# One of six low weight parts per expert step moved from VectorE to GpSimd

## The chip, the cores and the metric

One core of one Trainium2 chip runs the whole program. The metric is the device time of one execution in microseconds (us); less is better. The kernel before takes 1809.94 us (median of three runs, 1809.8 to 1809.99).

## The reference, cut to what matters

A hybrid block is followed by two more layers; the last of them ends in a mixture of experts. 256 tokens, 1024 wide, go through 8 experts of inner width 2816, and each token's two best experts count:

```python
def swiglu(x, w_gu, w_down):
    gu = jnp.einsum('bsd,df->bsf', x, w_gu)
    g, u = gu[..., :D_FF_2], gu[..., D_FF_2:]
    return jnp.einsum('bsf,fd->bsd', jax.nn.silu(g) * u, w_down)

def moe_swiglu(x, w_router, w_gu, w_down):
    ...
    for e in range(N_EXPERTS):
        out = out + gates[..., e:e + 1] * swiglu(x, w_gu[e], w_down[e])
    return out
```

All is float32. The kernel gets that precision from three fp32r products: every operand is split into a high part (rounded to fp32r) and a low part (the rest), and a product is high times high, plus low times high, plus high times low.

## The kernel before, in words

**The experts.** `expert` (L1579) runs once for each of 8 experts, 128 gathered tokens each, in 11 steps (j = 0 to 10) of 256 inner columns. A step reads three chunks of 1 MB from HBM with `load` (L181, issued by SP): two for gate and up weights, one for down weights. `split` (L187) makes two pairs from each chunk: the high part `wh` is a cast on ScalarE (L192), the low part `wl` is source minus high part on VectorE (L194), each 128x1024. So a step has six casts and six subtractions. The text calls the four pairs of the gate and up weights u0 to u3, and the two of the down weights d0 and d1; all six subtractions are VectorE's.

`up(j)` multiplies the tokens by u0 to u3 (24 matmuls of 512 columns, tile gu), takes silu on ScalarE (L1596), multiplies gate and up on VectorE (L1597, called mul below), transposes the product on TensorE (`tr`, L251) and splits it into hH (ScalarE, L1603) and hL (VectorE, L1604). `dnw` (L1607) loads and splits the down weights of the step before; `dn` (L1611) multiplies by them (12 matmuls, tile y; L241 is the one that reads a low part). An expert's last `dn` is run inside the next expert's first step, and its result goes through ScalarE (L1644) to HBM.

**Rings.** wh and wl live in five slots (rings "hl": 3 and 2), chunks in seven (rings "raw": 3, 1 and 3, after two lent ones are taken out in the first expert at JL = 8). A chunk's slot is free for the next load when its last reader, so far the subtraction of its second pair, is done.

**The gather.** Experts come in pairs. In experts 1, 3 and 5 the tokens of the next pair are gathered in four of the steps: matmuls into t (L1538, L1539), then xe on VectorE (L1543) and ScalarE (L1545, L1546), and its low part on GpSimd (L1547, 128x256, two in such a step). Besides these GpSimd has nothing to do in the experts, but for four indirect loads in the eighth (L1737).

**Order.** The order of the instructions on each engine is not written out: the program builder sorts them by its own estimate of when operands are ready, under the dependencies. `queue`, `behind` and `hold` add a few order constraints: `behind(..., 1)` keeps a subtraction on VectorE behind a held instruction; it acts while `held` is not used up, which is at the first few splits of a stage.

Of the kernel before, what the change touches and what calls it, by code (L numbers as in the profile page):

```python
# [8 lines left out]
F32 = mybir.dt.float32  # L9
# [108 lines left out]
def build(tc, a, out):  # L118
    nc = tc.nc
# [3 lines left out]
    def nm(s):  # L123
        uid[0] += 1
        return f"{s}_{uid[0]}"
# [21 lines left out]
    def slot(kind):  # L147

        p, taken = min(rings[kind], key=lambda x: x[1][0])
        count[0] += 1  # L150
        taken.append(count[0])
        taken.pop(0)
        return p
# [30 lines left out]
        nc.sync.dma_start(r[:, :n], ap.to_broadcast([128, n]) if ap.shape[0] == 1 else ap)  # L184
        return r

    def split(src):  # L187
        n = src.shape[-1]
        p = slot("hl")
        h = p.tile([128, CH // 2], F32R, tag="wh", name=nm("wh"))[:, :n]  # L190
        l = p.tile([128, CH // 2], F32R, tag="wl", name=nm("wl"))[:, :n]
        cast[0] = nc.scalar.copy(h, src)  # L192
        behind(cast[0], 0)
        behind(nc.vector.tensor_sub(l, src, h.bitcast(F32)), 1)  # L194
        count[1] += 1
        return h, l

# [9 lines left out]
    def behind(ins, i):  # L207
        if held[i] is not None and held[2] <= count[1]:
            queue(ins, held[i])
# [40 lines left out]
    def tr(o, i, k=128):  # L250
        nc.tensor.transpose(o, i, ident[:k, :k])  # L251
# [36 lines left out]
    with ExitStack() as st:  # L288
# [25 lines left out]
        for hf in range(2):  # L314
            c = slice(hf * 512, hf * 512 + 512)
# [41 lines left out]
    for k in range(8):  # L357
        if k % 2 == 0:
            h, l = split(bufs_[k // 4][:, (k % 4) * 280:(k % 4) * 280 + 560])
# [40 lines left out]
    for b in range(2):  # L400
# [3 lines left out]
        for h in range(8):  # L404
            o = bank("s", 3)
            r = slice(h % 2 * 64, h % 2 * 64 + 64)
# [15 lines left out]
        for kv in range(2):  # L422
# [3 lines left out]
            for i in range(4):  # L426
                h = kv * 4 + i
# [295 lines left out]
    for ch in (1, 2):  # L723
        c0 = BLK[ch][0]
# [40 lines left out]
    for ch in (1, 2):  # L765
        c0 = BLK[ch][0]
# [41 lines left out]
    for n in range(2):  # L808
        os_ = [bank("mm", 2) for _ in range(2)]
        for kg in range(2):  # L810
            r = load(a["w_z"][n * 2 + kg])
            for q in range(2):
                h, l = split(r[:, q * 1024:(q + 1) * 1024])
                for k2 in range(2):
                    k = kg * 4 + q * 2 + k2
                    s = slice(k2 * 512, k2 * 512 + 512)
                    for b in range(2):
                        c0 = BLK[b + 1][0]
# [474 lines left out]
    for b in range(2):  # L1293
        d = slice(b * 128, b * 128 + 128)
        o = bank("mm", 2)
        for k in range(8):
            h, l = hs[k // 2]
# [58 lines left out]
    for c in (0, 2):  # L1356
        hs = []
        for j in range(2):
            r = load(a["w_v"][c + j])
# [193 lines left out]
    made = pool("made", 1, bass.MemoryType.DRAM).tile([1024, D], F32, name="made")  # L1553
# [22 lines left out]
            nc.vector.tensor_reduce(rf, t, AX.X, ALU.add)  # L1576
            nc.vector.tensor_scalar_add(row[:, :, k], rf, C("own"))

    def expert(wap, xeH, xeL, c0, into=None, ST=None, gate=None, rest=None, ahead=(), final=False):  # L1579

        y = []

        def up(j):
            o = bank("gu", 2)
            for kg in range(2):
                r = load(wap(3 * j + kg))
                for q in range(2):
                    h, l = split(r[:, q * 1024:(q + 1) * 1024])  # L1590
                    for k2 in range(2):
                        k = kg * 4 + q * 2 + k2
                        s = slice(k2 * 512, k2 * 512 + 512)
                        xmm(o, xeH[:, k, c0:c0 + 128], xeL[:, k, c0:c0 + 128], h[:, s], l[:, s], k == 0, k == 7)
            g = ew.tile([128, 256], F32, tag="eg", name=nm("eg"))
            nc.scalar.activation(g, o[:, :256], AF.Silu)  # L1596
            mark[0] = nc.vector.tensor_mul(g, g, o[:, 256:])  # L1597
            t = bank("t", 2)
            for f in range(2):
                tr(t[:, f * 128:f * 128 + 128], g[:, f * 128:f * 128 + 128])  # L1600
            hH = ew.tile([128, 256], F32R, tag="hH", name=nm("hH"))
            hL = ew.tile([128, 256], F32R, tag="hL", name=nm("hL"))
            nc.scalar.copy(hH, t[:, :256])  # L1603
            nc.vector.tensor_sub(hL, t[:, :256], hH.bitcast(F32))  # L1604
            return hH, hL

        def dnw(j):  # L1607
            r = load(wap(3 * j + 2))
            return [split(r[:, f * 1024:(f + 1) * 1024]) for f in range(2)]

        def dn(j, hh, w=None, last=False):  # L1611
            w = w or dnw(j)
            if not y:
                y.extend(bank("y", 2) for _ in range(2))
            for f, n in ((0, 0), (1, 0), (0, 1), (1, 1)) if last else ((0, 0), (0, 1), (1, 0), (1, 1)):
                h, l = w[f]
                fs = slice(f * 128, f * 128 + 128)
                s = slice(n * 512, n * 512 + 512)
                xmm(y[n], hh[0][:, fs], hh[1][:, fs], h[:, s], l[:, s], j == 0 and f == 0, j == 10 and f == 1)

        pend = None
        for j in range(11):
            hh = up(j)
            w = dnw(pend[0]) if pend is not None else None
            if j < len(ahead):
                ahead[j]()
            if pend is not None:
                dn(*pend, w)
            pend = (j, hh)
            nj[0] += 1  # L1630
            if nj[0] == JL:
                rings["raw"][:] = [x for x in rings["raw"] if x not in lent]
            if rest is not None:
                rest(j)
        if final:
            dn(*pend, last=final)
            return y
        if into is not None:

            def store():  # L1640

                t = rowtile()
                for n in range(2):
                    queue(nc.scalar.copy(t[:, n * 512:n * 512 + 512], y[n]), cast[0])  # L1644
                nc.scalar.dma_start(into, t)

            return (lambda: dn(*pend)), store

        def sums(n):
            yy = rowtile().rearrange("p (i d) -> p i d", i=2).bitcast(F32R)  # L1650
            nc.scalar.copy(yy[:, 0], y[n])
            nc.vector.tensor_sub(yy[:, 1], y[n], yy[:, 0].bitcast(F32))
            s = slice(n * 512, n * 512 + 512)
            for b in range(2):
                o = bank("c", 2)
                for i in range(2):
                    mm(o, ST[:, b * 128:b * 128 + 128], yy[:, i], start=i == 0, stop=i == 1)
                nc.vector.scalar_tensor_tensor(x2[:, b, s], o, gate(b), x2[:, b, s], ALU.mult, ALU.add)

        return (lambda: dn(*pend)), (lambda: sums(0)), (lambda: sums(1))  # L1660
# [36 lines left out]
    left = ()  # L1697
# [8 lines left out]
    xe = tokens(0)  # L1706
    gather(*xe, S_, 2)
    for e in range(8):
        if e % 2 == 0 and e:
            xe, S_ = nxt  # L1710

        def rest(j, e=e):
            nonlocal nxt
            if e == 0 and j == 4:
                for n in range(2):
                    c = slice(n * 512, n * 512 + 512)
                    g, h = lnrow(0, n, "c"), lnrow(0, 2 + n, "c")
                    for b in range(2):
                        nc.vector.scalar_tensor_tensor(x2[:, b, c], xn[:, b, c], ALPHA, g, ALU.mult, ALU.mult)
                        nc.vector.scalar_tensor_tensor(x2[:, b, c], h, ALPHA, x2[:, b, c], ALU.mult, ALU.add)  # L1720
            if e == 1 and j < 4:
                nc.scalar.copy(gl_[:, j // 2, j % 2 * 512:j % 2 * 512 + 512], lnrow(1, j, "c"))

            if e % 2 and e < 7:
                if j == J0:
                    nxt = tokens(e + 1), ep.tile([128, 2, 2, 128], F32R, name=nm("S_"), tag="S", bufs=2)
                    onehot(nxt[1], pos, e + 1, 2)
                elif J0 < j <= J0 + 4:
                    k = 2 * (j - J0 - 1)
                    gather(*nxt[0], nxt[1], 2, k, k + 2)  # L1730
            if e == 2 and j == 0:
                places()

            if e == 7 and j in (2, 3, 6, 7):
                b, k = divmod(j - 2 if j < 4 else j - 4, 2)
                t = rowtile()
                nc.gpsimd.indirect_dma_start(t, None, made, bass.IndirectOffsetOnAxis(ap=row[:, b, k:k + 1], axis=0))  # L1737
                parts.append((b, k, t))
            if e == 7 and j in (5, 6, 9, 10):

                b, k, t = parts.pop(0)
                queue(nc.vector.scalar_tensor_tensor(x2[:, b], t, gk[:, b, k:k + 1], x2[:, b], ALU.mult, ALU.add), mark[0])
            if e == 6 and j == 5:
                o = bank("t", 2)
                for b in range(2):
                    sg = ew.tile([128, 128], F32, tag="sg", name=nm("sg"), bufs=1)
                    nc.vector.tensor_scalar_mul(sg, S_[:, b, 1].bitcast(F32), G[:, b, 7:8])
                    tr(o[:, b * 128:b * 128 + 128], sg)
                nc.scalar.copy(SG, o[:, :256])

        left = expert(lambda c, e=e: a["w_moe"][e * 33 + c], *xe, (e % 2) * 128, made[e * 128:e * 128 + 128], rest=rest, ahead=left, final=e == 7)
    y = left

    os_ = [bank(t, 2) for t in ("c", "c", "gu", "gu")]
# [15 lines left out]
    with tc.If(many > 128):  # L1770
# [3 lines left out]
        with tc.For_i(0, 8) as e:  # L1774
# [5 lines left out]
            xeH, xeL = [ew.tile([128, 8, 256], F32R, tag="xe" + n, name=nm("xe"), bufs=1) for n in "HL"]  # L1780
# [112 lines left out]
```

## Time and profile before

| | |
|---|---|
| median of runs | 1809.94 us |
| profiled execution, its own time | 1812.04 us |
| its span, first to last instruction | 1810.2 us |
| PE (matmul) busy | 1773.7 us, 98% |
| DVE (VectorE) busy | 1435.0 us, 79% |
| ACT (ScalarE) busy | 1129.9 us, 62% |
| POOL (GpSimd) busy | 136.0 us, 8% |
| the eight experts | from about 1012 to 1790 us of the span |
| granted TensorE clock, mean | 0.995 of 2.4 GHz |

The 88 steps of the experts are 43% of the span. An ordinary step lasts about 8.45 us, one with a gather about 9.7 us. A busy PE is a PE with a matmul in flight; matmuls overlap, so the spacing of their starts is what is read from a timeline.

### The profile page before, as it was taken

To read this page: it belongs to the slowest core of one execution; us is meant where nothing else is said; L and a number is where in the kernel's file an instruction comes from. 1 tells how busy PE (TensorE), PEld (TensorE's weight loads), DVE (VectorE), ACT (ScalarE), POOL (GpSimd) and SP (SyncE) were. 2 spreads that over 40 slices of the span, in tenths; PEclk is the share of its full clock that TensorE was granted. 3 is DMA by queue.
4 is the path that set the end of the run, shared out by engine and by line. 5 is a ranking of instruction groups with operands and counts; after the bars stand their busy time and mean duration, and the time that the engine had idled before them with its cause. 6 is when DMAs were issued, how large, how long until landed. Compare 5 with 4: busy or idle time off the path is not lost. (4 is left out here: it accounts for less than half of the span.)

```text
span 1810.2 us, 27298 instructions
## 1 busy us (share of the span) xinstructions
PE 1773.7 (98%) x10377; PEld 1515.8 (84%) x10377; DVE 1435.0 (79%) x2129; ACT 1129.9 (62%) x1704; POOL 136.0 (8%) x136
## 2 busy tenths in 40 slices
PE   9999999999999999999999899999999999999997
PEld 7978989999998898999977687888878787878775
DVE  6887886676666767555687999898989898989897
ACT  4477654564444655444454788887787777777775
POOL 2411220000000000000011200100010000100010
PEclk9999999999999999999999999999999999999999
DMA  6433331465554465553344689999999999999992
GB/s 224 171 102 113 105 137 61 176 250 202 186 186 166 166 218 224 209 189 137 117 163 164 239 334 373 331 365 347 374 353 355 361 379 366 349 354 377 366 414 94
DMA packets 64457, 443.45 MB, mean 245 GB/s; under 512 B 7952, under 2 KB 8368, under 8 KB 12608
## 3 DMA queue, kind: packets, MB, share of 16 engines
q1 hardware_dynamic: 59904, 430.04, 63.8%
q10 hardware_dynamic: 3840, 9.51, 1.4%
q8 instruction: 83, 1.36, 0.3%
q0 software_dynamic: 576, 2.10, 0.3%
q14 instruction: 54, 0.44, 0.1%
HBM read 436.37 MB, written 5.24 MB: 244 GB/s over the span
## 5 line engine op out<-in xcount | busy, mean ns | idle before, releaser
L194 DVE TENSOR_TENSOR wl<-raw,wh 128x1024 fp32r<-128x1024 f32 (+2 forms) x815 | 975.2, 1228 | 197.8 <-ACT wh L192 191.7
L192 ACT CAST wh<-raw 128x1024 fp32r<-128x1024 f32 (+2 forms) x815 | 824.6, 1047 | 338.1 <-PE mm L235 203.0
L239 PE MATMUL gu<-wh,xe 128*128 128x512 f32 x704 | 277.1, 394 | 0.8 <-DVE xe L1543 0.8
L240 PE MATMUL gu<-wh,xe 128*128 128x512 f32 x704 | 276.1, 392 | 1.3 <-POOL xe L1547 1.3
L241 PE MATMUL gu<-wl,xe 128*128 128x512 f32 x704 | 276.3, 393 | 0.0
L234 PE MATMUL mm<-xh,wh 128*128 128x256 f32 x592 | 168.2, 284 | 0.1
L235 PE MATMUL mm<-xl,wh 128*128 128x256 f32 x592 | 167.2, 282 | 0.0
L236 PE MATMUL mm<-xh,wl 128*128 128x256 f32 x592 | 166.7, 282 | 0.0
L241 PEld LDWEIGHTS gu<-wl,xe 128*128 128x128 f32 x704 | 132.2, 188 | 30.6 <-DVE wl L194 2.0
L240 PEld LDWEIGHTS gu<-wh,xe 128*128 128x128 f32 x704 | 132.3, 188 | 30.2 <-POOL xe L1547 2.7
L239 PEld LDWEIGHTS gu<-wh,xe 128*128 128x128 f32 x704 | 132.5, 188 | 27.4 <-DVE xe L1543 1.2
L239 PE MATMUL y<-wh,hH 128*128 128x512 f32 x352 | 139.3, 397 | 4.8 <-ACT yo L1644 4.8
L240 PE MATMUL y<-wh,hL 128*128 128x512 f32 x352 | 139.8, 397 | 0.0
L241 PE MATMUL y<-wl,hH 128*128 128x512 f32 x352 | 135.3, 405 | 0.0
L234 PEld LDWEIGHTS mm<-xh,wh 128*128 128x128 f32 x592 | 112.6, 190 | 4.4 <-issue 3.6
L235 PEld LDWEIGHTS mm<-xl,wh 128*128 128x128 f32 x592 | 112.4, 190 | 1.2 <-issue 0.8
L236 PEld LDWEIGHTS mm<-xh,wl 128*128 128x128 f32 x592 | 112.4, 190 | 0.0
L1596 ACT ACTIVATE eg<-gu 128x256 f32<-128x256 f32 x88 | 33.6, 382 | 107.6 <-PE gu L241 107.6
L234 PE MATMUL mm<-xTH,wh 128*128 128x256 f32 (+1 forms) x344 | 99.6, 290 | 0.6 <-DVE ct L384 0.5
L235 PE MATMUL mm<-xTL,wh 128*128 128x256 f32 (+1 forms) x344 | 98.8, 287 | 0.0
L236 PE MATMUL mm<-xTH,wl 128*128 128x256 f32 (+1 forms) x344 | 98.4, 286 | 0.0
L241 PE MATMUL acc<-wl,uh 128*128 128x512 f32 x216 | 85.1, 394 | 0.0
(573 smaller groups left out, 3275.8 us busy)
## 6 DMA issues: line engine op xcount, KB each, us to landing
raw<-w_moe SPq DMA_DIRECT2D x264, 1024.0 KB, 6.3
raw<-w_gud SPq DMA_DIRECT2D x33, 1024.0 KB, 4.8
raw<-w_ffn SPq DMA_DIRECT2D x32, 1024.0 KB, 4.8
raw<-w_wf SPq DMA_DIRECT2D x27, 1024.0 KB, 4.8
raw<-w_a SPq DMA_DIRECT2D x10, 1024.0 KB, 4.9
raw<-w_br SPq DMA_DIRECT2D x8, 1024.0 KB, 4.8
raw<-w_o SPq DMA_DIRECT2D x8, 1024.0 KB, 4.8
raw<-w_b SPq DMA_DIRECT2D x7, 1024.0 KB, 4.7
```

The lines of the kernel that those rows point to most:

```text
L192: cast[0] = nc.scalar.copy(h, src)
L194: behind(nc.vector.tensor_sub(l, src, h.bitcast(F32)), 1)
L234: mm(o, h[:, k], xh[:, k, ts], start=k == 0, stop=False)
L235: mm(o, h[:, k], xl[:, k, ts], start=False, stop=False)
L236: mm(o, l[:, k], xh[:, k, ts], start=False, stop=k == 7)
L239: mm(o, xh, h, start=first, stop=False)
L240: mm(o, xl, h, start=False, stop=False)
L241: mm(o, xh, l, start=False, stop=last)
L1596: nc.scalar.activation(g, o[:, :256], AF.Silu)
```

## The change

`split` gets a flag by which the subtraction goes to GpSimd; `dnw` sets it for the second half of the chunk (f = 1, so d1), and the caller for experts 0 to 6. `behind` is not called for it. Nothing else in the source is changed.

```diff
-    def split(src):
+    def split(src, pool=False):
...
-        behind(nc.vector.tensor_sub(l, src, h.bitcast(F32)), 1)
+        if pool:
+            nc.gpsimd.tensor_sub(l, src, h.bitcast(F32))
+        else:
+            behind(nc.vector.tensor_sub(l, src, h.bitcast(F32)), 1)
...
-    def expert(wap, xeH, xeL, c0, into=None, ST=None, gate=None, rest=None, ahead=(), final=False):
+    def expert(wap, xeH, xeL, c0, into=None, ST=None, gate=None, rest=None, ahead=(), final=False, third=False):
...
-            return [split(r[:, f * 1024:(f + 1) * 1024]) for f in range(2)]
+            return [split(r[:, f * 1024:(f + 1) * 1024], f == 1 and third) for f in range(2)]
...
-        left = expert(lambda c, e=e: a["w_moe"][e * 33 + c], *xe, (e % 2) * 128, made[e * 128:e * 128 + 128], rest=rest, ahead=left, final=e == 7)
+        left = expert(lambda c, e=e: a["w_moe"][e * 33 + c], *xe, (e % 2) * 128, made[e * 128:e * 128 + 128], rest=rest, ahead=left, final=e == 7, third=e < 7)
```

## Rows read from the trace of the kernel before

**Rows 1.** Busy time of each engine by stretch: early steps, one late step, gather step, step with expert change
```profile
core 0: us, PE busy (x) PEld busy (x) DVE busy (x) ACT busy (x) POOL busy (x), PEclk, DMA share, GB/s
1179.80:1222.30 42.50, 42.50 (x191) 34.31 (x190) 39.76 (x41) 34.06 (x41) 0.00 (x0) 1.00 0.97 373
1306.30:1314.80 8.50, 8.50 (x40) 6.96 (x40) 7.81 (x9) 6.49 (x9) 0.00 (x0) 1.00 0.97 372
1343.10:1352.80 9.70, 9.70 (x48) 7.68 (x47) 8.51 (x10) 7.89 (x11) 2.56 (x2) 1.00 0.89 329
1314.80:1324.50 9.70, 8.75 (x40) 6.87 (x39) 7.97 (x10) 7.87 (x12) 0.00 (x0) 1.00 0.93 344
```

**Rows 2.** Waits from 1100 to 1800 us: us in total, times, longest us
```profile
ACT eg L1596 <- PE gu L241: 107.6, 66, 3.5
...
PEld y L239 <- ACT yo L1644: 6.9, 5, 1.4
PE y L239 <- ACT yo L1644: 4.8, 5, 1.0
...
PEld gu L241 <- DVE wl L194: 2.0, 7, 0.4
...
PEld y L241 <- DVE wl L194: 0.8, 4, 0.2
```

**Rows 3.** Timeline of an ordinary late step: start us, us, engine, line, xcount, idle before
```profile
1306.58 3.90 ACT L192 CAST wh<-raw 128x1024 fp32r<-128x1024 f32 x4
...
1307.67 4.63 DVE L194 TENSOR_TENSOR wl<-raw,wh 128x1024 fp32r<-128x1024 f32 x4
...
1312.29 1.99 ACT L192 CAST wh<-raw 128x1024 fp32r<-128x1024 f32 x2
...
1312.42 0.42 DVE L1597 TENSOR_TENSOR eg<-eg,gu 128x256 f32<-128x256 f32 x1
...
1313.36 2.36 DVE L194 TENSOR_TENSOR wl<-raw,wh 128x1024 fp32r<-128x1024 f32 x2 [0.51 <-ACT wh L192]
...
1314.10 0.40 PE L241 MATMUL y<-wl,hH 128*128 128x512 f32 x1
```

**Rows 4.** GpSimd's timeline in the experts: two subtractions of 128x256
```profile
1161.99 0.74 POOL L1547 TENSOR_TENSOR xe<-eg,xe 128x256 fp32r<-128x256 f32 x1 [6.34 <-ACT eg L1546]
...
1346.78 1.82 POOL L1547 TENSOR_TENSOR xe<-eg,xe 128x256 fp32r<-128x256 f32 x1 [1.60 <-ACT eg L1546]
```

**Rows 5.** VectorE beside them: hL at 1161.89, and L194 from 1200 to 1400 us (min/median/max)
```profile
1161.89 0.42 DVE L1604 TENSOR_TENSOR hL<-t,hH 128x256 fp32r<-128x256 f32 x1
...
L194 DVE TENSOR_TENSOR wl<-raw,wh x136: 1207/1218/1765, 1198.8 to 1399.4; 128x1024 fp32r<-128x1024 f32 x136
```

**Rows 6.** Timeline, GpSimd's 128x512 operations in an earlier stage, and VectorE beside the second
```profile
217.20 1.28 POOL L740 TENSOR_TENSOR kT<-kT,t 128x512 f32<-128x512 f32 x1
...
265.90 1.22 DVE L194 TENSOR_TENSOR wl<-raw,wh 128x1024 fp32r<-128x1024 f32 x1
...
266.06 2.21 POOL L826 TENSOR_TENSOR zg<-zg,rows 128x512 f32<-128x512 f32 x1 [0.73 <-DVE zg L825]
```

**Rows 7.** Timeline of a late gather step
```profile
1345.19 0.54 DVE L1543 TENSOR_SCALAR xe<-t,ge 128x256 fp32r<-128x256 f32 x1 [1.19 <-PE t L1539]
...
1347.92 2.90 DVE L194 TENSOR_TENSOR wl<-raw,wh 128x1024 fp32r<-128x1024 f32 x2
...
1351.00 0.19 PEld L241 LDWEIGHTS y<-wl,hH 128*128 128x128 f32 x1
```

**Rows 8.** Timeline of an ordinary early step
```profile
1203.68 0.39 PE L241 MATMUL y<-wl,hH 128*128 128x512 f32 x1
...
1204.37 2.50 DVE L194 TENSOR_TENSOR wl<-raw,wh 128x1024 fp32r<-128x1024 f32 x2
...
1207.29 5.34 DVE L194 TENSOR_TENSOR wl<-raw,wh 128x1024 fp32r<-128x1024 f32 x4
```

**Rows 9.** Loads (L184) from 1200 to 1700 us, from issue to landing
```profile
DMA to landing us min/median/max: 4.7/6.5/8.7
```

## The prediction

> **What bounds the kernel now.** I read the stretches of the experts first, because the change touches nothing else. In early steps and in an ordinary late step PE is busy for the whole stretch, with VectorE at 39.76 of 42.50 us and 7.81 of 8.50 us [rows 1]. The waits say the same: ScalarE waits 107.6 us for PE, VectorE's subtractions make PE wait 2.0 us (gu) and 0.8 us (y) in 700 us, and the one large wait of PE is for ScalarE's copy of y, five times [rows 2]. So PE is the bound, and VectorE, 92% busy, is hidden. Taking work from VectorE can return the 2.8 us of the two small waits at most, unless the order of the queues changes with it. What has to be asked is whether the new GpSimd work stays hidden too.
>
> **What is removed.** 77 subtractions (7 experts of 11 steps) leave VectorE. One is 1.22 us long, and 1.14 us apart in a run of four, (4.63 - 1.22) / 3 [rows 3]. That frees some 1.14 us of each step on an engine that does not bound: worth 0 to 2.8 us in all.
>
> **What is added: 77 GpSimd subtractions of 128x1024.** No row shows one. By length: 0.74 us for 256 columns with no rival [rows 4] and 1.28 us for 512 [rows 6], so 0.54 us for each 256 and 1.28 + 2 x 0.54 = 2.36 us alone. By what it takes from VectorE: the 256-column one at 1346.78 lasted 1.82 us, not 0.74, since it had to let the VectorE subtraction in flight end [rows 4]; then the longest VectorE subtraction came to 1.765 us against a median of 1.218 [rows 5]. The two don't run beside each other: one holds the other off for its whole length, 0.55 us for 256 columns, so 2.19 us for 1024. The 512-column one at 266.06 ended at 268.27, 1.15 us after VectorE's subtraction at 265.90 (end 267.12) [rows 6], which makes 2.30 us for 1024. I take 2.2 us (the row with the same operation in the same stage), bounds 2.19 and 2.36 us. An operation that reads one of its inputs from PSUM isn't held off: hL took 0.42 us beside a GpSimd subtraction that took its 0.74 us [rows 4, 5]; mul, one input from PSUM as well, counts likewise.
>
> The Trainium skill (GPSIMD Engine Reference, "Key points") states that GpSimd shares its SBUF interfaces with VectorE and conflicts with VectorE instructions that have two SBUF inputs; rows 4 and 5 agree, with 1.82 against 0.74 us. The same page (section "Engine selection") says to keep elementwise work on VectorE, as about 2 times slower on GpSimd; by that rule the change loses, which is the second rival below.
>
> **An ordinary late step** (experts 2 to 6, no gather). VectorE's order is u0, u1, hL, u2, u3, d0, d1, mul. The run of four from 1307.67 is u2 to d1, so d0 ends at about 1311.16 and d1 at 1312.30; its cast ends at 1310.48, and PE reads d1 first at 1314.10 [rows 3], its weights some 0.23 us (one matmul's spacing) before. GpSimd would begin when d0 lets go, 1311.16, and end at 1313.36. That is 0.5 us before PE's weight load. In these 2.2 us VectorE has only mul to do, which doesn't conflict; the next subtraction starts at 1313.36 as it is, since its cast is not ready sooner [rows 3]. The gap fits the lock almost exactly. Cost 0. With 2.36 us u0 is 0.16 us late, and a late start can be made up: five subtractions at 1.14, hL at about 0.34 and 2.2 us of lock make 8.25 us (8.4 with 2.36), under the 8.45 us of PE. Cost 0 again, with 0.05 to 0.2 us to spare.
>
> **Early steps** (experts 0 and 1, start of 2). Low parts are made far ahead: PE runs d0's first L241 at 1203.68, before this step's d0 and d1 are made from 1204.37 [rows 8]; those are for the next y, a step later. mul stands between u3 and d0. d1 would end near 1207.9, 1 us later than now, against a lead of over 5 us; u0 at 1207.29 waits some 0.5 us, and the run of four at 5.34 us has 5.34 - 4.63 = 0.7 us of air [rows 3, 8]. Cost 0.
>
> **Late gather steps** (four in expert 3, four in expert 5). Here the cover is thin. The two subtractions from 1347.92 are d0 and d1, and they end at 1350.82; PE loads d1's weights at 1351.00 [rows 7], 0.18 us later. d0 ends at about 1349.68, so GpSimd would end at 1351.88: PE waits 0.9 us. This isn't made up, because the next run of subtractions follows L1543, which waits for PE itself [rows 7]. Over the other such steps I read the same distance as 0.1 to 0.35 us: waits of 0.7 to 1.0 us, eight times, 7 us. That holds if the order of the queues is kept. The builder sorts by its own estimates, and it does react: in the early step L241 follows its own pair of matmuls directly, in the ordinary late steps it stands behind both pairs [rows 3, 8]. If it takes GpSimd's part for late, it puts other matmuls before it, and the 7 us shrink, to 0 at best. The expert 1 gather has the early lead. I take 1 us.
>
> **Loads.** A down chunk's slot comes free 1.05 us later. Seven slots at three chunks per 8.45 us turn over in 19.7 us, a load lands in 6.5 us, 8.7 at worst [rows 9]; working a chunk takes some 3 us. 8 us are left: 0. SP's queue, in which later loads stand behind the waiting one, is late by the same 1 us. GpSimd's queue holds only L1547 in these steps, whose result the next pair of experts needs.
>
> **Sum.** The profiled execution took 1812.04 us (span 1810.2 and 1.8 around it), 2.1 us over the median. 77 x 0 + 1 us: 1813.0 us against it, and 1811 us against the median.
>
> **The rivals.**
> (1) *The gather steps wait in full*: the order stays there, PE waits 7 us (0.7 to 1.0 us eight times): 1817 us. For it: the margin of 0.18 us [rows 7]. Against: a reordering that looks as in [rows 3].
> (2) *The lock is the bound*. Slower: VectorE gives 1.14 us and loses 2.2 us of access, so its chain in a step is 8.25 us where PE needs 8.45. It decides when the lock passes 2.4 us; every 0.1 us over that costs 0.1 us in some 55 ordinary steps of experts 0 to 6 without slack, 5.5 us. At 2.5 to 2.8 us: 1816 to 1832 us. Against: 256 and 512 columns both scale to under 2.4 us [rows 4 to 6].
> (3) *VectorE stays ahead*: with a sixth less on it in the builder's plan, the early order lasts through expert 6. What this is worth: an expert change costs 9.70 us in place of 8.45 [rows 1] because ScalarE's copy of y comes after silu (five waits, [rows 2]); the two changes in the early stretch have no such wait. 5 x 1.25 = 6 us, and about 1 us in gather steps: 1803 us. For it: the two orders exist in one kernel. Against: nothing in the trace says that the builder's own estimate of VectorE ends the early order.
> (4) *The change doesn't do what it says*: for experts 0 to 6 the flag is set on one call of each step, so this has no chance worth a number.
>
> **How the numbers follow.** A measurement of this kernel tells about 0.2% (3.6 us) from no change. Forecast, all covered but for 0 to 3.6 us: 0.41. Rival 1: 0.22. Rival 2: 0.13. Rival 3: 0.24. So faster 0.24 (rival 3), same 0.41, slower 0.35 (rivals 1 and 2). The range takes in rival 3 to 1803 us, rival 1, and of rival 2 what a lock just past its point costs, to 1820 us; left out are the rest of rival 2 and the far end of rival 3. The forecast's own range is 1807 to 1813.5 us.
>
> **What would show it.** GpSimd has 77 subtractions at L194's neighbour line, 2.2 to 2.4 us each where VectorE lets go at once; VectorE's busy time in the late stretch falls by about 1.1 us a step, its longest subtractions grow by up to the lock. Ordinary steps stay at 8.45 us. Rival 1: waits of PE's L241 for GpSimd, 0.7 to 1.0 us, in experts 3 and 5 alone. Rival 2: ordinary steps over 8.5 us, PE waiting for wl everywhere. Rival 3: no wait of y for ScalarE's copy at an expert change. The forecast is wrong if the ordinary step changes at all, either because the lock isn't proportional to the columns or because the builder gives the queues an order of which nothing here knows.

## The result: 12.8 us slower

The changed kernel takes 1822.66 us (median of six runs, 1820.9 to 1823.65) where the kernel before took 1809.87 us beside it: a ratio of 1.007, interval 1.0057 to 1.0083. The prediction was 1811 us within 1803 to 1820 us, so the result lies outside the range, on its slower side. The profiled execution of the changed kernel took 1821.15 us (span 1819.1), the one of before 1812.04 (span 1810.2).

In all views below, lines after 194 stand three lines lower than before: the matmuls are L242 to L244, the transposes L254, silu L1599, mul L1600, hL L1607. GpSimd's low part is L195, VectorE's L197.

Much of what the prediction said of the single pieces holds; its gather steps don't. The windows of three steps, an ordinary late one, a gather step and a change of expert (columns as in [rows 1]; the granted clock is 1.00 in all three, as before):

```profile
1310.20:1318.70 8.50, 8.50 (x39) 6.95 (x38) 6.67 (x8) 6.45 (x9) 3.06 (x1) 1.00 0.96 360
1347.40:1357.40 10.00, 9.93 (x48) 7.60 (x47) 8.01 (x9) 7.89 (x11) 5.02 (x3) 1.00 0.84 315
1318.70:1328.40 9.70, 8.75 (x40) 6.85 (x39) 7.00 (x9) 8.20 (x12) 3.03 (x1) 1.00 0.97 350
```

VectorE's busy time in the ordinary step falls from 7.81 to 6.67 us, the 1.14 us of the forecast, and the step still takes 8.5 us. The gather step has grown from 9.70 to some 10.05 us. The change of expert still takes 9.7 us [rows 1]. In the ordinary step GpSimd's operation lies where the forecast put it: mul passes beside it, and VectorE's next subtraction is held for only 0.1 us (timeline):

```profile
1314.46 3.06 POOL L195 TENSOR_TENSOR wl<-raw,wh 128x1024 fp32r<-128x1024 f32 x1 [5.48 <-ACT wh L192]
...
1316.34 0.42 DVE L1600 TENSOR_TENSOR eg<-eg,gu 128x256 f32<-128x256 f32 x1 [1.09 <-ACT eg L1599]
...
1317.28 1.32 DVE L197 TENSOR_TENSOR wl<-raw,wh 128x1024 fp32r<-128x1024 f32 x1 [0.52 <-ACT wh L192]
```

The group of GpSimd's subtractions (min/median/max in ns), with who waited for it, and then VectorE's subtractions and its 88 muls:

```profile
L195 POOL TENSOR_TENSOR wl<-raw,wh x77: 2384/3027/5847, 1026.9 to 1707.0; 128x1024 fp32r<-128x1024 f32 x77
...
who waited for it (us, times):
  PEld y L244: 5.4, 9
  PE y L244: 1.1, 4
```
```profile
L197 DVE TENSOR_TENSOR wl<-raw,wh x441: 1206/1219/3431, 1029.7 to 1798.5; 128x1024 fp32r<-128x1024 f32 x147
...
L1600 DVE TENSOR_TENSOR eg<-eg,gu x88: 403/421/423, 1028.6 to 1797.0; 128x256 f32<-128x256 f32 x88
```

2.38 us is GpSimd's own time (estimated: 2.36). A VectorE subtraction that meets it grows from 1.22 to 3.43 us, so the lock (the time for which GpSimd's operation holds such a VectorE operation off) is 2.2 us, as estimated [rows 4, 5]. Not one mul is longer than 0.42 us. But the median of GpSimd's is 3.03 and the longest is 5.85 us: it waits for VectorE. In 76 of the 77 it waits at most for the operation in flight; once it let three more subtractions pass.

The waits of TensorE from 1100 to 1804.5 us, against [rows 2]:

```profile
PEld y L242 <- ACT yo L1647: 6.9, 5, 1.4
...
PEld t L254 <- DVE eg L1600: 5.3, 17, 1.1
PEld y L244 <- POOL wl L195: 4.9, 8, 0.8
PE y L242 <- ACT yo L1647: 4.8, 5, 1.0
...
PEld gu L244 <- DVE wl L197: 2.4, 8, 0.4
PEld y L244 <- DVE wl L197: 2.0, 2, 1.0
```

The five waits for the copy of y are unchanged: no trace of the third rival. New are eight waits for GpSimd's low part, the first rival's, and 5.3 us in seventeen waits of the transposes (t) for mul (eg); no part of the prediction had these. In the trace of before (1100 to 1800 us) they were:

```profile
PEld t L251 <- DVE eg L1597: 1.5, 7, 0.2
```

Late loads are no part of the loss: between 1020 and 1790 us the loads now wait for GpSimd's reading of their slots as well, but no cast shows a wait for a load.

**Where the time went.** I cut both traces at the first matmul of each of the 88 steps and subtract. In what follows a step carries its number j, 0 to 10. Executions reach expert 0 at times between 1009.7 and 1013.8 us although nothing before it differs, and step 0 of expert 0 took 0.67 us more than in the profile of before in every kernel but one, those with unchanged expert 0 among them; so I count from step 2 of expert 0 on. The sum is 10.8 us, within the interval of the ratio (10.3 to 15.0 us).

| us over before, by expert | 0 | 1 | 2 | 3 | 4 | 5 | 6 | 7 | sum |
|---|---|---|---|---|---|---|---|---|---|
| the change | 3.85 | 1.38 | 0.58 | 2.60 | 0.17 | 2.30 | -0.28 | 0.18 | 10.8 |

Of expert 0's 3.85 us the steps 2 to 5 lose 3.6. Expert 1 loses 0.8 in the steps 2 and 3 and 0.9 in its last gather step, 6, where the longest of the waits for mul lies, 1.1 us; 0.4 comes back in step 7. Of expert 3's 2.60 the four gather steps lose 1.5 and the step after them 0.9, and expert 5 does the same. Ordinary late steps lose 0.09 us each at most: expert 4, all ordinary, loses 0.17 us.

**The start of expert 0.** Before, in the timeline of the third step (VectorE, silu and the transposes):

```profile
1035.94 5.76 DVE L194 TENSOR_TENSOR wl<-raw,wh 128x1024 fp32r<-128x1024 f32 x5
...
1041.80 0.37 ACT L1596 ACTIVATE eg<-gu 128x256 f32<-128x256 f32 x1
...
1042.20 0.42 DVE L1597 TENSOR_TENSOR eg<-eg,gu 128x256 f32<-128x256 f32 x1 [0.50 <-ACT eg L1596]
...
1042.88 0.38 PE L251 MATMUL t<-cst,eg 128*128 128x128 f32 x2
```

VectorE has done its subtractions, pauses for 0.50 us, and does mul at once when silu ends. The same place in the changed kernel (its step 2 starts 1.9 us earlier in its own execution):

```profile
1034.11 9.11 DVE L197 TENSOR_TENSOR wl<-raw,wh 128x1024 fp32r<-128x1024 f32 x6
...
1035.15 5.85 POOL L195 TENSOR_TENSOR wl<-raw,wh 128x1024 fp32r<-128x1024 f32 x1 [5.81 <-ACT wh L192]
...
1039.94 0.37 ACT L1599 ACTIVATE eg<-gu 128x256 f32<-128x256 f32 x1
...
1043.14 0.41 DVE L1600 TENSOR_TENSOR eg<-eg,gu 128x256 f32<-128x256 f32 x1
...
1043.69 0.41 PE L254 MATMUL t<-cst,eg 128*128 128x128 f32 x2 [1.44 <-DVE eg L1600]
```

Six subtractions at 1.14 us would take 6.9 us; they take 9.11, 2.2 us more. GpSimd began at 1035.15 during the first of them, let three more pass before it, and held the one after them off. Silu ended at 1040.31; mul began at 1043.14, 2.8 us later, since it stands behind the delayed subtractions; TensorE waited 1.44 us for it. Mul itself, with an input in PSUM, takes its usual 0.41 us. It isn't held off; it queues behind work that is.

### The profile page after: what moved, and what is told of

The parts are those of the page before. It is cut to its first block, busy times and chain, and to the rows that moved or that the text cites. A ratio compares the mean times of both kernels' runs of the same rounds, so it can differ in the third digit from the quotient of the medians.

```text
span 1819.1 us, 27328 instructions
## 1 busy us (share of the span) xinstructions
PE 1774.7 (98%) x10372; PEld 1513.3 (83%) x10377; DVE 1382.7 (76%) x2052; ACT 1131.1 (62%) x1704; POOL 359.2 (20%) x213
## 3 DMA queue, kind: packets, MB, share of 16 engines
q8 instruction: 84, 1.38, 0.3%
## 5 line engine op out<-in xcount | busy, mean ns | idle before, releaser
L197 DVE TENSOR_TENSOR wl<-raw,wh 128x1024 fp32r<-128x1024 f32 (+2 forms) x738 | 917.2, 1271 | 221.0 <-ACT wh L192 218.9
L195 POOL TENSOR_TENSOR wl<-raw,wh 128x1024 fp32r<-128x1024 f32 x77 | 223.7, 2905 | 399.6 <-ACT wh L192 386.1
L242 PE MATMUL gu<-wh,xe 128*128 128x512 f32 x704 | 277.8, 395 | 0.8 <-DVE xe L1546 0.8
L244 PE MATMUL gu<-wl,xe 128*128 128x512 f32 x704 | 277.0, 394 | 0.0
L244 PEld LDWEIGHTS gu<-wl,xe 128*128 128x128 f32 x704 | 132.3, 188 | 32.5 <-DVE wl L197 2.4
L242 PEld LDWEIGHTS gu<-wh,xe 128*128 128x128 f32 x704 | 132.3, 188 | 27.5 <-DVE xe L1546 1.2
L242 PE MATMUL y<-wh,hH 128*128 128x512 f32 x352 | 139.2, 396 | 4.8 <-ACT yo L1647 4.8
L244 PE MATMUL y<-wl,hH 128*128 128x512 f32 x352 | 134.6, 400 | 2.6 <-DVE wl L197 1.1
L1599 ACT ACTIVATE eg<-gu 128x256 f32<-128x256 f32 x88 | 33.7, 382 | 105.8 <-PE gu L244 105.8
```

The lines of the kernel that those rows point to most:

```text
L195: nc.gpsimd.tensor_sub(l, src, h.bitcast(F32))
L242: mm(o, xh, h, start=first, stop=False)
L244: mm(o, xh, l, start=False, stop=last)
```

## The experiments

Three theories went into them. A: the loss is the lock, and what it costs depends on what stands in VectorE's queue where it falls. B: it is the later result, TensorE waiting for GpSimd. C: it is the other order in which the builder, which plans with an emptier VectorE, puts the queues. Kernels of one group ran beside the kernel before (medians 1810.5 to 1811.0 us).

**By place.** Four kernels give GpSimd the part only in some experts or steps.

The cuts show only the argument that differs.

```diff
-third=e < 7
+third=e == 0             # only_e0
+third=e in (1, 3, 5)     # only_e135
+third=e in (2, 4, 6)     # only_e246
```
```diff
-return [split(r[:, f * 1024:(f + 1) * 1024], f == 1 and third) for f in range(2)]
+return [split(r[:, f * 1024:(f + 1) * 1024], f == 1 and j in third) for f in range(2)]
-third=e < 7
+third=() if e == 7 else range(4 if e == 0 else 6 if e % 2 else 0, 11)
```

> GpSimd makes d1's low part in expert 0 alone (11 of the 77). Theory A, the lock where VectorE has no pause (start of expert 0, and gather steps): the first five steps lose what they lost in the change, about 4.5 us: 1814.5 us. Theory B, GpSimd's slower subtraction makes every d1 late by the same: 12.8 / 7 = 1.8 us per expert: 1811.7 us. Theory C, the builder's other order costs the time, not the lock: PE's order differs from before in some 20 of 10534 matmuls here, so within 1 us of before: 1810 to 1811 us.

> GpSimd makes d1's low part in experts 1, 3 and 5 alone, the ones with a gather in them. A: 1.5 + 2.4 + 2.3 = 6.2 us, as these experts lost in the change: 1816 us. B: 3 x 1.8 = 5.5 us, 1815.4 us, spread over all eleven steps of each. C: PE's order differs by some 90 matmuls, about half as many as in the whole change: 6 us, but then the experts 2, 4, 6 alone, with as many moved, cost as much.

> GpSimd makes d1's low part in experts 2, 4 and 6 alone: no gather, no start. A: 0 to 1 us (ordinary steps lost 0 to 0.08 us each): 1810 to 1811 us. B: 3 x 1.8 = 5.5 us: 1815.4 us. C: as much as experts 1, 3, 5 alone, some 6 us: 1816 us.

> As the change, but VectorE keeps d1's low part in the first four chunks of expert 0 and in the first six of experts 1, 3 and 5 (where the gather lies): 55 of the 77 stay on GpSimd. A: 0 to 2 us: 1810 to 1812 us. B: 55 / 77 of 12.8 = 9.1 us: 1819 us. C: PE's order still differs from before by over 100 matmuls, 6 us or more: 1816 us.

| | us | ratio (interval) | by expert 0 to 7, us over before | sum |
|---|---|---|---|---|
| only_e0 | 1813.48 | 1.0017 (1.0008 to 1.0026) | 3.80, -0.05, -0.06, 0.13, 0, 0.01, -0.01, 0.01 | 3.8 |
| only_e135 | 1815.65 | 1.0028 (1.0018 to 1.0039) | 0.06, 1.46, -0.05, 2.45, 0.04, 2.44, 0.09, 0.02 | 6.5 |
| only_e246 | 1811.89 | 1.0005 (0.9996 to 1.0014) | 0.02, -0.20, 0.91, 0.08, 0.21, 0.05, -0.32, 0.01 | 0.8 |
| skip | 1815.62 | 1.0023 (1.0014 to 1.0032) | 2.74, -0.19, 0.99, 0.24, 0.41, 0.20, -0.20, 0.10 | 4.3 |

The first three add up: 3.8 + 6.5 + 0.8 = 11.1 us against 10.8 us for the whole change. B, the same price everywhere, falls: 33 of the 77 cost 0.8 us in all, 11 cost 3.8. So does the simple form of C. And skip missed: I expected 0 to 2 us. Its gather steps lose nothing, but expert 0's loss isn't gone, it has moved: from the steps 2 to 5 to the steps 6 and 7 (1.90 + 0.86 us), just behind the point from which GpSimd makes the part. So in expert 0 it isn't the steps 2 to 5 as such that cost, but the place where GpSimd's work comes in. Expert 2 doesn't fit that so simply: in skip and in only_e246 it loses 0.9 us in its step 7, long after GpSimd's first operation there. In only_e246 TensorE waits 1.0 us there for a VectorE subtraction; why just there I didn't follow.

In skip, GpSimd's first operation of expert 0 (1059.78 us) costs nothing. Its second falls on the small VectorE operations of onehot, which the builder has put there (timeline):

```profile
1069.47 2.48 POOL L195 TENSOR_TENSOR wl<-raw,wh 128x1024 fp32r<-128x1024 f32 x1 [7.27 <-ACT wh L192]
...
1069.58 2.65 DVE L1503 TENSOR_SCALAR S__2174_12214<-cst,pos 128x128 fp32r<-128x128 f32 x2
```

Two of them, 0.28 us each elsewhere, take 2.65 us. Mul and the rest of the queue stand behind them.

**The order of the start put back.** As only_e0, with two subtractions kept behind mul as they stood before (`sub[0]` is the subtraction just issued, `mark[0]` the last mul).

```diff
 h, l = split(r[:, q * 1024:(q + 1) * 1024])
+if (nj[0], 2 * kg + q) in ((3, 2), (4, 3)):
+    queue(sub[0], mark[0])
```

> As expert 0 alone (3.1 us slower than before), with two subtractions of VectorE kept behind the mul of the step before in VectorE's queue, where before had them: u3.2 behind mul 2, u4.3 behind mul 3. If the loss needs both, the mul placed behind two subtractions and the lock that stretches one of them, it goes down to under 1 us: 1811 us, and the steps 2 to 4 of expert 0 take 11.5, 8.5 and 9.3 us as before. If the lock alone makes it, 2.2 us of it stay: 1813 us.

1814.43 us, ratio 1.0017 (1.0007 to 1.0027), the steps 2 to 5 lose 3.7 us: no gain at all, against both expectations. The timeline shows why:

```profile
1034.54 4.61 DVE L197 TENSOR_TENSOR wl<-raw,wh 128x1024 fp32r<-128x1024 f32 x4
...
1035.61 5.82 POOL L195 TENSOR_TENSOR wl<-raw,wh 128x1024 fp32r<-128x1024 f32 x1 [5.84 <-ACT wh L192]
...
1039.07 2.40 DVE L1577 SCALAR_TENSOR_TENSOR rsel<-rk,rok 128x14 f32<-128x14 f32 x1
```

In the room that the subtraction left, the builder put small operations ahead of mul; GpSimd again let the run of subtractions pass, and now an operation of 14 columns took 2.40 us (0.16 us before). The 2.2 us fall on whatever comes next that can be held off.

**The same order, another GpSimd operation.** A copy of the raw piece, which needn't wait for ScalarE's cast, in place of the subtraction; the result then lacks the right low part of d1.

```diff
-nc.gpsimd.tensor_sub(l, src, h.bitcast(F32))
+nc.gpsimd.tensor_copy(l, src)
```

> As the change, with the same order on every engine, but each of the 77 GpSimd operations is a copy of the raw piece (one input from SBUF) in place of the subtraction (two); the y of experts 0 to 6 lack the right low part. Theory A, the lock: if GpSimd's one-input operation doesn't hold VectorE off, VectorE's subtractions stay at 1.22 us and most of the loss goes: 1810 to 1814 us. If the copy holds it off too, the time stays near 1822 us and VectorE still shows subtractions of over 3 us. Theory C, the order of the queues: the order is the same, so the loss stays: 1820 to 1823 us, without long subtractions. Theory B, the latency of GpSimd: falls with the copy's length.

1838.34 us, ratio 1.0147 (1.013 to 1.0164): slower than the change, which no theory had expected, though the operation takes 1.04 us instead of 2.38. By expert it is the reverse of the change: the steps 2 to 5 lose only 0.5 us in place of 3.6 with the very same order of the queues, but an ordinary late step loses 0.77 us in place of 0.05 (timeline of a step):

```profile
1300.46 1.04 POOL L195 CAST wl<-raw 128x1024 fp32r<-128x1024 f32 x1 [8.18 <-PE y L244]
...
1300.57 3.14 DVE L197 TENSOR_TENSOR wl<-raw,wh 128x1024 fp32r<-128x1024 f32 x2 [0.26 <-ACT wh L192]
...
1302.63 0.19 PEld L244 LDWEIGHTS gu<-wl,xe 128*128 128x128 f32 x1 [0.88 <-DVE wl L197]
```

The copy starts as soon as its slot is free ([8.18 <-PE y]), and that moment falls 0.1 us ahead of u1, whose low part TensorE needs next. The two subtractions take 3.14 us instead of 2.35, and TensorE waits 0.88 us. So a GpSimd operation with one input holds VectorE off too, and 0.8 us of lock at that place costs some fifteen times what 2.2 us cost behind d0. This is theory A in its sharpest form.

**The lock alone, in ordinary steps.** The kernel before, and one GpSimd subtraction more per step in experts 2, 4 and 6, whose result nobody reads (`again` is set for d1 there).

```diff
 behind(nc.vector.tensor_sub(l, src, h.bitcast(F32)), 1)
+if again:
+    nc.gpsimd.tensor_sub(src, src, h.bitcast(F32))
```

> The kernel before, with its order unchanged on every engine, and in experts 2, 4 and 6 a GpSimd subtraction of 128x1024 more per step, of d1's piece over its own raw piece, after VectorE's; nobody reads it. Lock: VectorE's work in an ordinary step is six subtractions at 1.14, hL and mul at 0.34 each and 2.2 us of lock, 9.7 us, where PE needs 8.45: some 30 steps at 1.25 us, less the lead at the start of expert 2: 30 to 41 us slower, with VectorE's next subtraction at over 3 us. No lock: within 2 us of before (the raw piece's slot comes free 2.4 us later, against 8 us of air).

1842.44 us, one run; the steps lose 30.6 us, inside the 30 to 41 us of the lock. The queues have the order of before, and 33 operations cost 0.93 us each, 1.1 us in a steady step. Only the loads wait for GpSimd, which reads and writes their slots, and from 1200 to 1800 us no cast shows a wait for a load. This kernel leaves all six subtractions on VectorE, so it shows what the lock costs when its time is not made free: by the sum in the expectation VectorE then has more to do than a step of TensorE lasts. In the timeline, two subtractions that would take 2.35 us take 3.51, since the first meets the rest of GpSimd's 2.42:

```profile
1438.36 2.42 POOL L196 TENSOR_TENSOR raw<-raw,wh 128x1024 f32<-128x1024 f32 x1 [7.17 <-DVE wl L194]
...
1439.49 3.51 DVE L194 TENSOR_TENSOR wl<-raw,wh 128x1024 fp32r<-128x1024 f32 x2 [0.52 <-ACT wh L192]
...
1441.91 0.19 PEld L243 LDWEIGHTS gu<-wl,xe 128*128 128x128 f32 x1 [0.81 <-DVE wl L194]
```

**Half the lock.** In experts 1, 3 and 5 GpSimd makes 512 of the 1024 columns.

```diff
+c = n // 2
+behind(nc.vector.tensor_sub(l[:, :c], src[:, :c], h[:, :c].bitcast(F32)), 1)
+nc.gpsimd.tensor_sub(l[:, c:], src[:, c:], h[:, c:].bitcast(F32))
```

> As experts 1, 3 and 5 alone (5.1 us slower than before), but GpSimd makes only the second half of d1's low part (512 columns, for the second half of y), VectorE the first. If the lock's length decides, it halves to 1.1 us and the gather steps lose less than half: 1811 to 1812.5 us. If it is the latency of d1, the second half is read later by two matmuls (0.46 us) and comes 1.1 us sooner: no wait at all, 1810.5 us. If it is the order, 1813 us or more.

1822.27 us, ratio 1.006 (1.0044 to 1.0077): more than twice the loss of only_e135 by medians (10.6 us in place of 6.5 by steps), where two of the three theories expected less. The gather steps lose 2.7 and 2.6 us in place of 1.6 and 1.4, and ordinary late steps 0.4 to 0.5 us in place of 0.05. One of these:

```profile
1406.07 1.95 POOL L197 TENSOR_TENSOR wl<-raw,wh 128x512 fp32r<-128x512 f32 x1 [6.92 <-ACT wh L192]
...
1406.79 1.78 DVE L196 TENSOR_TENSOR wl<-raw,wh 128x512 fp32r<-128x512 f32 x1
...
1408.50 0.41 DVE L1602 TENSOR_TENSOR eg<-eg,gu 128x256 f32<-128x256 f32 x1
```

VectorE's half (L196) stands between GpSimd's operation and mul (L1602), meets the lock and takes 1.78 us, and mul comes after it. With the whole part on GpSimd only mul stands there, which passes. So half the lock can cost more, by what stands behind it. The half also leaves VectorE one instruction more and has an order of its own; these weren't taken apart.

**The lock and the later result, taken apart.** First nobody makes d1's low part; then GpSimd makes it, and nobody reads it. The order is the same in both, on every engine; the change's own differs from it in a few operations of experts 0 to 2.

```diff
-nc.gpsimd.tensor_sub(l, src, h.bitcast(F32))
+l = h
```
```diff
 nc.gpsimd.tensor_sub(l, src, h.bitcast(F32))
+l = h
```

> As the change, but nobody makes d1's low part in experts 0 to 6 (the matmuls read the high part a second time in its place; the y of these experts lack the right low part): VectorE is freed of the 77 subtractions and GpSimd adds nothing. If the loss of the change is GpSimd's (its lock on VectorE and its later result), this runs at the time of before or a little under it: 1807 to 1811 us, with expert 3's gather steps at 9.7 us and the start of expert 0 as before. If the loss is the order that the builder makes of an emptier VectorE, it stays: 1816 us or more. If freed VectorE time were worth something, the 2.8 us of PE's two small waits would show as 1807 to 1808 us.

> As the kernel in which the matmuls read the high part a second time (1809.5 us), with the same order on every engine, but GpSimd does make its 77 low parts; nobody reads them (the y of experts 0 to 6 lack the right low part). So the lock on VectorE is there and the later result costs nothing. If the whole loss is the lock: 1820 to 1822 us. If all of it is PE waiting for GpSimd's result: 1809 to 1811 us. By the places seen in the change: the start of expert 0 and expert 1 (about 5 us) are VectorE's mul held up by the lock and stay, the gather steps of experts 3 and 5 (4.7 us) are PE waiting for GpSimd's low part and go: 1814 to 1816 us.

no_low_part: 1809.49 us, ratio 0.9994 (0.9985 to 1.0004). VectorE with a sixth less to do is worth nothing that the times can tell, and the builder's order for it costs nothing either. By steps one thing is gained: step 6 of expert 6, 9.15 us long before, is 0.5 us shorter, as it is in the change. unread: 1819.38 us, ratio 1.005 (1.0036 to 1.0064), more than the 1814 to 1816 us that I expected. By steps it is +10.1 us where no_low_part is -0.5: GpSimd's operation alone makes 10.6 us (10.1 by the ratios), though nobody reads its result. The steps 2 to 5 of expert 0 are 3.6 us over before with it and 0.15 us under without, in one and the same order: theory C falls, and the start is the lock's. Here too no cast shows a wait for a load, and no VectorE operation one for GpSimd, so what is left for the operation to act by is the lock. Reading GpSimd's part adds 10.8 - 10.1 = 0.7 us by steps (3.6 us by the ratios, whose intervals overlap). That is a balance of two sides: experts 3 and 5 together lose 2.5 us unread and 4.9 us in the change, so there about half of the loss is the wait for the later result; experts 0 to 2 lose 7.6 us unread and 5.8 us in the change, whose order isn't quite the same there. TensorE's waits from 1010 to 1800 us, first without the part, then with the part unread:

```profile
PE y L242 <- ACT yo L1647: 4.7, 5, 0.9
PE gu L243 <- POOL xe L1550: 1.8, 5, 0.7
```
```profile
PE t L255 <- DVE eg L1601: 5.2, 7, 1.8
PE y L243 <- ACT yo L1648: 4.7, 5, 0.9
PE gu L244 <- POOL xe L1551: 1.8, 5, 0.7
```

The largest wait that the unread operation adds is the one of the transposes (t) for mul (eg), up to 1.8 us at a time. The expectation of 1814 to 1816 us failed at two places. Experts 0 and 1 lose 6.6 us in place of some 5. And in the gather steps of experts 3 and 5 the wait for GpSimd's part does go, but the lock's price then shows in the step behind them, 1.54 and 1.36 us in place of 0.88 and 0.85 in the change. There that step reads so (timeline):

```profile
1380.42 2.62 POOL L195 TENSOR_TENSOR wl<-raw,wh 128x1024 fp32r<-128x1024 f32 x1 [4.46 <-ACT wh L192]
...
1384.17 0.30 PEld L244 LDWEIGHTS y<-wl,hH 128*128 128x128 f32 x2 [0.99 <-DVE wl L197]
```

VectorE has fallen behind in the gather, the cast of d1 is done before VectorE gets to d0, GpSimd comes in ahead of d0, and TensorE, which needs d0 first, waits 0.99 us for it.

**Something to do with the freed time.** The largest wait that the profile shows is TensorE's for ScalarE's copy of y, so half of that copy went to VectorE, in the kernel before and in only_e246.

```diff
-queue(nc.scalar.copy(t[:, n * 512:n * 512 + 512], y[n]), cast[0])
+yo = t[:, n * 512:n * 512 + 512]
+if n:
+    nc.vector.tensor_copy(yo, y[n])
+else:
+    queue(nc.scalar.copy(yo, y[n]), cast[0])
```

> The kernel before, with the second half of each expert's copy of y made by VectorE in place of ScalarE: the five waits of PE for that copy are the largest wait that the profile of before shows. If ScalarE's two copies one after the other set the wait, half of it goes: up to 0.7 us at each of five expert changes, 1807 us. If VectorE's copy stands behind other work in its full queue, nothing is gained or it is slower: 1811 to 1816 us.

> As experts 2, 4 and 6 alone (0.9 us over before), with the second half of the copy of y on VectorE, whose time GpSimd frees there. If the freed time makes room for the copy, the expert changes lose up to 0.7 us each: 1808 us, better than both kernels. If the lock of GpSimd falls on the copy or on what stands around it, no gain: 1811 us or more.

1813.12 us, ratio 1.0015 (1.0006 to 1.0025), and 1814.08 us, 1.0015 (1.0005 to 1.0024): both slower, by 0.15%. The first gains 0.28 us at the change from expert 2 to 3 and loses 0.96 us in the next step; TensorE's weight loads wait 1.2 us for the copy in place of 6.9, but 5.7 us for ScalarE's casts and 7.4 us for VectorE's subtractions (2.0 before, [rows 2]), which come behind it. The second gains 1.1 us at the changes to experts 4 and 6, where GpSimd has freed VectorE, and gives back 0.8 and 0.7 us a step later; at the changes to experts 3, 5 and 7 it loses 0.9 us each. No version here beats the kernel before, and no_low_part says why: what can be had from VectorE's load in this place is at most 0.0015 of the time, 2.7 us, if the part cost nothing at all.

## Why the prediction was wrong

- **Removed work, 0 to 2.8 us**: right; no_low_part shows 0.9994.
- **GpSimd's 2.36 us and the lock of 2.2 us**: right (2.38; 3.43 - 1.22 = 2.2). That mul and hL aren't held off is right too.
- **An ordinary late step, cost 0**: right within 0.09 us [rows 3]. The gap behind d0 fits the lock, by luck of what stands there: with one subtraction of 512 columns between it and mul, half the lock costs 0.4 to 0.5 us a step (half_e135), and a GpSimd copy that comes in 0.1 us ahead of u1 costs 0.77 us (copy).
- **"Early steps ... Cost 0"**: this is the step that failed first, with 3.85 us in expert 0, 1.4 in expert 1 and 0.4 in one step of expert 2. I read one step in the middle of the early stretch, where the lead is over 5 us [rows 8], and let it stand for the start, where the lead has yet to be made and VectorE works back to back. The sum in it ("0.7 us of air") counted the lock as one wait between two subtractions; I didn't ask what stands behind in VectorE's queue. It is mul, and for mul TensorE waits: 1.44 us at once in expert 0, 1.1 us in expert 1, whose gather I had also covered with the early lead.
- **"GpSimd would begin when d0 lets go"**: holds where VectorE pauses after d0. Against subtractions back to back it let three pass (5.85 us).
- **The gather steps, 7 us or 0, taken as 1**: this term was mis-sized: the eight lose 2.9 us and the two steps behind them 1.7, 4.6 us in place of 1. The first rival's mechanism is there, TensorE waits for GpSimd's part in experts 3 and 5, at 0.3 to 0.4 us a step instead of 0.7 to 1.0. The step behind, where the lock falls on d0, was in no part of the text.
- **The rivals**: the mechanism of 1 happened at under half its size; 2, the lock as a bound of every step, did not, nor 3 (the five waits stand). Of the second the runs show the condition: with nothing taken from VectorE the lock does bound the ordinary step (dummy_e246). The range ended at 1820 us because the lock had a price in one place only, where VectorE's chain fills the step. It has one wherever something that TensorE needs queues behind it.
- **The builder**: I feared its order. unread and no_low_part have one order and differ by 10.6 us, so the order alone isn't the cost; no_low_part, with that order and no lock, runs at the time of before.

What stays open: GpSimd's exact moment of entry in a run of VectorE operations. The traces show it behind the operation in flight in 76 of the change's 77, and now and then behind more: three in the change, one in pin_e0, two in unread. No experiment varied that alone. Open too is expert 2's loss of 0.9 us in step 7 in skip and only_e246.

## What to carry to other kernels

Before work goes to GpSimd beside a busy VectorE, don't ask whether it is hidden on average but what stands in VectorE's queue behind the moment at which GpSimd will get in, and who waits for that, at the start of the stage and in its irregular steps as well as in an ordinary one. Here the engine that wasn't the bound had no time worth giving away. Two kernels tell that: one that leaves the moved work out altogether bounds the gain (0.9994), and one in which GpSimd does it and nobody reads it shows the price (1.005).

## What the runs showed of the hardware that I had not expected

- GpSimd can wait through several VectorE operations, though it rarely did (one of the change's 77): 5.85 us for a subtraction of 2.38 us, with three VectorE subtractions passing first; the next one was then held for the whole 2.2 us.
- The hold isn't one of large subtractions alone: a VectorE operation of 14 columns took 2.40 us in place of 0.16, and two of onehot's of 128 columns 2.65 us, where one is 0.28 us. The Trainium skill (GPSIMD Engine Reference, "Key points") tells of conflicts with VectorE instructions that have two SBUF inputs; the row of 14 columns, which has two (rk and rok), agrees with its 2.40 us. In both rows the price is GpSimd's length, not the VectorE operation's.
- A GpSimd copy with one input, 1.04 us for 1024 columns, holds VectorE's subtraction off as well (3.14 us for two in place of 2.35).
